# The first layer's convolution: from three element-wise engines to float32 products on TensorE

## The chip, the cores and the metric

One core of one Trainium2 chip runs the whole program. The metric is the device time of one execution in microseconds. A core has TensorE (PE in the profile; PEld are its weight loads), VectorE (DVE), ScalarE (ACT), GpSimd (POOL) and SyncE (SP, which issues most of the DMAs here). They run side by side and wait for each other by semaphores. Each takes its own instructions in the order in which the program lists them.

## The reference, cut to what matters

The model has two layers over 256 latent tokens and 256 context tokens, of width 1024. The first layer normalizes and modulates its input, projects it once, and splits the result into a convolution branch (values `a`, gates `g`, 512 channels each) and grouped-query attention (8 query heads, 2 key heads, of 64). Both results are joined and projected back.

```python
def _conv_branch(a, g, conv_w, ln_g, ln_b):
    y = a * jax.nn.sigmoid(g)
    pad = CONV_WIDTH // 2
    y = lax.conv_general_dilated(y, conv_w[:, None, :].astype(y.dtype), (1,), [(pad, pad)],
                                 dimension_numbers=('NWC', 'WIO', 'NWC'), feature_group_count=CONV_CH)
    return jax.nn.silu(_layer_norm(y, ln_g, ln_b))
...
    y_l = jnp.concatenate([conv_l, att_l], axis=-1) @ w_out
```

The convolution is per channel: 31 taps along the tokens, separately for latent and context tokens. The layer norm goes over the 512 channels of a token. After this come a dense SwiGLU, then the second layer with differential attention and a top-2-of-8 expert SwiGLU, and a last norm. All is float32.

## The kernel before, in words

Weights are streamed from HBM in tiles of 1 MB by `Stream`: `load` issues a DMA, `split` (ScalarE, L140) and `low` (VectorE, L152) make a rounded high part and a low part of a tile, and `mm3` (L222) forms a product as high x high, high x low and low x high, at the fast rate of the type F32R. `ws.step()` lets the stream split one tile more. `ws.get` forces splits until the wanted one is there. The DMAs and the splits go in the order in which a first pass over the program asks for the tiles.

The order of the work around the change is written out by hand in `build`:

1. The shifted, scaled input `hT` is made, and the first half of gates and values is projected with it (blocks j = 0, 1 of 128 channels); gated, they lie in `ypad` (128 channels x 4 blocks x 2 streams x 286 padded tokens).
2. The keys and values of the attention are projected (`kv_proj`), normed and rotated (`kv_a`, `kv_b`), and turned (`kv_T`).
3. The queries likewise, in four tiles of 128 tokens (`q_proj`, `q_a`, `q_b`, `q_T`).
4. Attention runs over 32 units (a tile of tokens and a head) in a software pipeline: scores (`ev_A`), maximum, exponential, transposes (`ev_C`), high and low parts, product with the values (`ev_D`), division by the sums (`ev_E`). The generator `ag1` puts the second half of gates and values (j = 2, 3) between these units. `fill` does the same with later adaLN rows, in `ada_half` (L334): float32 products with 32 output columns, in four column groups.
5. The output projection `w_out` takes eight blocks k of joined channels: 0 to 3 from the convolution, 4 to 7 from attention. It goes through them in the order kk = 2, 3, 0, 1 of pairs.

The convolution runs beside steps 2 to 4 on the element-wise engines. `conv_v` has taps 0 to 12 on VectorE, a multiply and add each:

```python
nc.vector.scalar_tensor_tensor(cacc[:, j], ypad[:, j, :, w:w + 256], cw[:, j, w:w + 1], cacc[:, j],
                               op0=OP.mult, op1=OP.add)
```

`conv_p` has taps 13 to 30: ScalarE makes the product (L581), GpSimd adds it (L599). The calls `conv(p, v)` scattered through the code say how many steps of either are issued there. Its layer norm (`conv_ln`) follows from inside the attention loop: transposes to tokens, bn_stats, scaling. The SiLU (`conv_silu`) comes with transposes back at the start of the output projection.

PSUM has eight banks, by tags: "mm" four, "tr" two, "av" and "ad" one each. A tag's next user waits until the one before has been read.

Of the kernel before, what the change touches and what calls it, by code (L numbers as in the profile page):

```python
# [10 lines left out]
F32 = mybir.dt.float32  # L11
# [3 lines left out]
OP = mybir.AluOpType  # L15
# [180 lines left out]
def build(nc, tc, a, out, order, dbg=None, stop=None):  # L196
# [5 lines left out]
    def T(shape, name, dt=F32, tag=None, bufs=1):  # L202
        return pool.tile(shape, dt, name=name, tag=tag or name, bufs=bufs)
# [65 lines left out]
    dq(rows[16:20], a["ev_ln_g"].rearrange("b (k p) -> (b k) p", p=128))  # L269
    dq(rows[20:24], a["ev_ln_b"].rearrange("b (k p) -> (b k) p", p=128))  # L270
# [275 lines left out]
    cacc = T([128, 4, 2, 256], "cacc", tag="cB")  # L546
    NP = 18
    cpool = {}

    ready = set()  # L550

    def conv_v():
        for j in range(4):
            while j not in ready:
                yield
            nc.vector.tensor_scalar(cacc[:, j], ypad[:, j, :, 0:256], cw[:, j, 0:1], None, op0=OP.mult)
            yield
            for w in range(1, 31 - NP):
                nc.vector.scalar_tensor_tensor(cacc[:, j], ypad[:, j, :, w:w + 256], cw[:, j, w:w + 1], cacc[:, j],
                                               op0=OP.mult, op1=OP.add)  # L560
                yield
            while (j, "done") not in cpool:
                yield
            nc.vector.tensor_tensor(cacc[:, j], cacc[:, j], cpool[j].rearrange("p (s n) -> p s n", s=2), op=OP.add)
            cpool[j, "added"] = True
            yield

    def conv_p():

        todo = [(j, w) for j in range(4) for w in range(31 - NP, 31)]  # L570
        cps = T([128, 2, 512], "cps", tag="s4")
        prod = {}

        def product(i):
            j, w = todo[i]
            first = w == 31 - NP
            if first or i % 2:
                o = pool.tile([128, 512], F32, name="cp", tag="ptlo" if first else "pthi", bufs=2)
            else:
                o = cps[:, i // 2 % 2]  # L580
            nc.scalar.activation(o.rearrange("p (s n) -> p s n", s=2), ypad[:, j, :, w:w + 256], AF.Copy,  # L581
                                 scale=cw[:, j, w:w + 1])
            if first:
                cpool[j] = o
            prod[i] = o

        made = 0
        for i, (j, w) in enumerate(todo):
            while made < min(i + 3, len(todo)):
                j1, w1 = todo[made]  # L590
                if w1 == 31 - NP and (j1 not in ready or j1 >= 2 and (j1 - 2, "added") not in cpool):
                    if made > i:
                        break
                    yield
                else:
                    product(made)
                    made += 1
            if w > 31 - NP:
                nc.gpsimd.tensor_tensor(cpool[j], cpool[j], prod.pop(i), op=OP.add)  # L599
            if w == 30:  # L600
                cpool[j, "done"] = True
            yield

    convg, convp = conv_v(), conv_p()

    def conv_rest():
        while run(convg, 1):
            run(convp, 2)

    def conv(p, v):  # L610
        return run(convp, p) | run(convg, v)

    def latent(p):
        return p.rearrange("p (s n) -> p s n", s=2)

# [3 lines left out]
    def gated(j, pa):  # L619

        y = ypad[:, j, :, 15:271]
        nc.vector.tensor_tensor(y, latent(pa), y, op=OP.mult)
        ready.add(j)
# [6 lines left out]
    def ag1():  # L630

        for i in (1, 0):
            u = ag_w(i, 1)
            for j in (2, 3):
                o = PS("ad")
                ag_mm(o, u, j, range(4))
                yield
                yield
                ag_mm(o, u, j, range(4, 8))
                if j == 3:  # L640
                    ws.done(("win", i, 1), 0, 1)
                yield
                (gate_to if i == 1 else gated)(j, o)
                yield

    ag2 = ag1()


# [25 lines left out]

    kT = [T([128, 2, 512], f"k{q}", F32R, tag=f"b{4 + q}") for q in range(2)]
# [83 lines left out]
    conv(2, 1)  # L759
# [3 lines left out]
    conv(1, 1)  # L763
# [4 lines left out]
    conv(1, 1)  # L768
# [3 lines left out]
    ws.fewer(spares)  # L772
    ws.done(("win", 3, 0), 0, 1)
    bq = [PS("av"), PS("mm"), PS("mm"), PS("mm")]
# [3 lines left out]
    conv(1, 1)  # L778
    kv_b(2)
    kv_a(3)  # L780
    q_proj(0)
    kv_b(3)
    conv(1, 0)
    q_a(0)
    kv_T(0)()
    conv(0, 1)
    q_b(0)
    conv(2, 1)
    q_proj(1)
    q_a(1)  # L790
    kv_T(2)()
    conv(0, 1)
    q_b(1)
    conv(2, 1)
    q_proj(2)
    q_a(2)
    q_T(0)()
    conv(0, 1)
    q_b(2)
    conv(2, 1)  # L800
    for k in range(8):
        mm3(bq[3], [x[:, k, 384:512] for x in hT], [x[:, k % 2, :] for x in un[k // 2]], k == 0, k == 7)
        if k % 2:
            ws.done(("win", 2, k // 4), k // 2 % 2)
            ws.step()
    q_a(3)
    q_T(1)()
# [13 lines left out]
    run(ag2, 4)  # L821
# [86 lines left out]
    yn = {}  # L908

    def conv_ln():  # L910
        yn[0] = T([128, 4, 512], "yn", tag="cA")
        mv = T([128, 4, 2], "mv")
        for t in range(4):
            p = PS("tr")
            for j in range(4):
                tr(p[:, j * 128:(j + 1) * 128], cacc[:, j, t // 2, (t % 2) * 128:(t % 2) * 128 + 128])
            yield
            nc.scalar.copy(yn[0][:, t], p)
            bs = SM(6, "bs")
            nc.vector.bn_stats(bs, p)  # L920
            nc.vector.bn_aggr(mv[:, t], bs)
            yield
        r = powm(mv[:, :, 1], 4, 1.0, 1e-5)
        yield
        for t in range(4):
            nc.vector.tensor_scalar(yn[0][:, t], yn[0][:, t], mv[:, t, 0:1], r[:, t:t + 1], op0=OP.subtract,
                                    op1=OP.mult)

    def conv_silu():
        for j in range(4):  # L930
            p = PS("tr")
            for t in range(4):
                tr(p[:, t * 128:(t + 1) * 128], yn[0][:, t, j * 128:(j + 1) * 128])
            cs = W("cs")
            nc.scalar.activation(cs, p, AF.Silu, scale=lnT[:, j:j + 1], bias=lnT[:, 4 + j:5 + j])
            parts(cat[0][:, j, :], cat[1][:, j, :], cs)
            yield

    ws.lag = 5
    lng = conv_ln()  # L940
    n = len(units)
    evs = None
    for i in range(n + 8):
        if 0 < i < 7:
            run(ag2, 1)
        if i < n:
            ev_A(i)
        if 3 <= i < n + 3:
            ev_C(i - 3)
        if 2 <= i < n + 2:  # L950
            ev_exp(i - 2)
        if evs is not None:
            run(evs, 1)
        if 1 <= i < n + 1:
            ev_max(i - 1)
        if 4 <= i < n + 4:
            ev_parts(i - 4)
        if 5 <= i < n + 5:
            ev_D(i - 5)
            if i % 4 == 0:  # L960
                evs = ev_E((i - 5) // 8, (i - 5) // 4 % 2)
        run(qlast, 1)
        ws.step()
        rest = conv(2, 1 + i % 2)
        if i < 6:
            run(ag2, 1)
        if i == 9:
            run(ag2)
            cat[:] = new_h("cat")
        if i >= 9:  # L970
            fill(2 if i >= 16 and i % 3 == 0 else 1)
        if i >= 34:
            conv_rest()
            rest = False
        if not rest:
            run(lng, 1 + i % 2)
# [4 lines left out]
    conv_rest()  # L981
    run(lng)
    fill(10 ** 6)
    ws.lag = 0
    sil = conv_silu()
# [14 lines left out]
    run(sil, 1)  # L1000
# [13 lines left out]
    for i, kk in enumerate((2, 3, 0, 1)):  # L1014
        un = w_out_w(0, kk)
        for t in range(4):
            w_out(0, kk, t, bo[t], un, i == 0, i == 3)
        ws.done(("wout", 0, 0, kk // 2), kk % 2)
        ws.step()
        run(sil, 2)  # L1020
        if i >= 1:
            run(gg, 2)
        fill(2)
# [3 lines left out]
    uns = {kk: w_out_w(1, kk) for kk in (2, 3, 0, 1)}  # L1027
    fillers += [ada_half(0, 5, 1)]
    for t in range(4):
        bank = PS("mm")  # L1030
        for i, kk in enumerate((2, 3, 0, 1)):
# [839 lines left out]
_INS = ['x', 'c', 'ctx', 'c_ctx', 'ada_b', 'norm1_g', 'norm2_g', 'ev_conv_w', 'ev_ln_g', 'ev_ln_b', 'ev_q_norm_g',  # L1871
# [13 lines left out]
def weights(v):  # L1885
# [8 lines left out]
    out["t_win"] = np.stack([wide[0:2], wide[2:4], q, np.stack([wide[6], wide[6]])])  # L1894
    wo = [blocks(v[n][0], 512, 512).transpose(1, 0, 2, 3) for n in ("ev_w_out", "od_w_out")]
# [51 lines left out]
```

## Time and profile before

| | us |
|---|---|
| median of 3 runs | 2074.19 (2070.69 to 2074.53) |
| profiled execution | 2073.23 |
| its span, first to last instruction | 2071.4 |
| TensorE busy | 1984.1 |
| VectorE busy | 1539.5 |
| ScalarE busy | 1185.9 |
| GpSimd busy | 336.1 |

The span is what the trace covers; the execution's own time is 1.8 us longer. Busy time counts only instructions that compute, and a matmul's end is modelled, so a busy TensorE is not one at its peak. [...]

### The profile page before, as it was taken

The page shows a single profiled execution, that of the slowest core. Times are in us where ns is not written, and L with a number is a line of the kernel's source. Part 1 is how long each engine was busy: PE and PEld are TensorE (multiplying, and loading weights), DVE is VectorE, ACT ScalarE, POOL GpSimd, SP SyncE. Part 2 cuts the span into 40 slices and gives each one's busy share as a digit, 9 for nine tenths or more (in the row PEclk, how much of TensorE's full clock was granted, in tenths as well). Part 3 has the DMA queues.
Part 4 walks back from the last instruction along what each step waited for, and adds up shares of the span by engine and source line. Part 5 has one row for each costly group of instructions (what it writes and reads, how often), then busy time and mean ns, then how long its engine had stood idle before and what let it go on. Part 6 is the DMA issues. An engine that isn't in the chain of part 4 may idle for free.

```text
span 2071.4 us, 26926 instructions
## 1 busy us (share of the span) xinstructions
PE 1984.1 (96%) x9910; PEld 1609.1 (78%) x9910; DVE 1539.5 (74%) x1965; ACT 1185.9 (57%) x1635; POOL 336.1 (16%) x285
## 2 busy tenths in 40 slices
PE   6999899999999998999999999999999999999987
PEld 4766677777777776889878888888888888888876
DVE  3789643545546466666559999999999999999997
ACT  3467433222222222434458888878788888888776
POOL 0568210333324243011110000000000000000020
PEclk9999699999999999999889999999999999999999
DMA  8315332333332223332397999999999999999972
GB/s 300 117 42 202 124 136 107 143 122 125 125 131 94 81 99 120 126 123 102 127 337 289 354 359 353 359 361 373 360 346 364 372 367 352 356 358 375 352 304 96
DMA packets 98632, 483.28 MB, mean 233 GB/s; under 512 B 12169, under 2 KB 12833, under 8 KB 51648
## 3 DMA queue, kind: packets, MB, share of 16 engines
q1 hardware_dynamic: 96128, 479.84, 62.7%
q10 hardware_dynamic: 2368, 1.68, 0.3%
q8 instruction: 79, 1.29, 0.3%
q14 instruction: 57, 0.47, 0.1%
HBM read 480.43 MB, written 1.05 MB: 232 GB/s over the span
## 4 chain that ended last, share of the span: by engine, by line
PE 57%; DVE 2%; ACT 1%; issue 0%; DVEq 0%; POOL 0%; ACTq 0%; POOLq 0%
PE mm L223 12%; PE mm L225 12%; PE mm L224 12%; PE av L224 3%; PE av L225 3%; PE av L223 3%; PE ad L225 2%; PE ad L223 2%; PE ad L224 2%; PE tr L308 2%; DVE wlo L152 1%; PE tr L1636 1%; PE tr L1562 1%; PE tr L1514 0%; PE av L1448 0%
## 5 line engine op out<-in xcount | busy, mean ns | idle before, releaser
L140 ACT CAST whi<-raw 128x1024 fp32r<-128x1024 f32 x420 | 434.7, 1049 | 232.8 <-PE tr L225 102.7
L152 DVE TENSOR_TENSOR wlo<-raw,whi 128x1024 fp32r<-128x1024 f32 x420 | 547.5, 1342 | 9.6 <-ACT whi L140 7.7
L224 PE MATMUL mm<-wlo,xghi 128*128 128x512 f32 x896 | 351.3, 392 | 5.1 <-DVE wlo L152 5.0
L223 PE MATMUL mm<-whi,xghi 128*128 128x512 f32 x896 | 354.6, 396 | 0.0
L225 PE MATMUL mm<-whi,xglo 128*128 128x512 f32 x896 | 351.2, 392 | 0.0
L990 POOL TENSOR_TENSOR x<-x,tmp 128x512 f32<-128x512 f32 x110 | 163.3, 1516 | 387.8 <-DVE tmp L989 356.8
L140 ACT CAST whi<-spare 128x512 fp32r<-128x512 f32 (+1 forms) x282 | 189.1, 709 | 45.0 <-PE mm L225 27.4
L152 DVE TENSOR_TENSOR wlo<-spare,whi 128x512 fp32r<-128x512 f32 (+1 forms) x282 | 212.3, 794 | 0.0
L224 PEld LDWEIGHTS mm<-wlo,xghi 128*128 128x128 f32 x896 | 168.9, 188 | 43.5 <-DVE wlo L152 8.4
L225 PEld LDWEIGHTS mm<-whi,xglo 128*128 128x128 f32 x896 | 168.7, 188 | 36.4
L223 PEld LDWEIGHTS mm<-whi,xghi 128*128 128x128 f32 x896 | 168.9, 188 | 34.6
L223 PE MATMUL mm<-h2hi,whi 128*128 128x512 f32 x448 | 178.2, 398 | 1.0 <-ACT h2hi L228 1.0
L224 PE MATMUL mm<-h2lo,whi 128*128 128x512 f32 x448 | 177.3, 396 | 0.6 <-DVE h2lo L229 0.5
L225 PE MATMUL mm<-h2hi,wlo 128*128 128x512 f32 x448 | 176.8, 395 | 0.0
L1088 DVE TENSOR_TENSOR silu<-mm,silu 128x512 f32<-128x512 f32 x28 | 19.4, 692 | 191.7 <-PE mm L225 191.7
L1649 POOL MEMSET fgain<- 128x1 f32 x1 | 0.1, 98 | 899.3 <-DVE wlo L152 899.3
L152 DVE TENSOR_TENSOR wlo<-rawx,whi 128x1024 fp32r<-128x1024 f32 x112 | 134.3, 1221 | 3.1 <-ACT whi L140 0.7
L140 ACT CAST whi<-rawx 128x1024 fp32r<-128x1024 f32 x112 | 117.4, 1052 | 31.0 <-PE mm L225 25.7
L223 PEld LDWEIGHTS mm<-h2hi,whi 128*128 128x128 f32 x448 | 84.0, 187 | 24.3 <-issue 3.4
L224 PEld LDWEIGHTS mm<-h2lo,whi 128*128 128x128 f32 x448 | 84.0, 188 | 21.5 <-DVE h2lo L229 1.6
L225 PEld LDWEIGHTS mm<-h2hi,wlo 128*128 128x128 f32 x448 | 84.1, 188 | 20.0
L223 PE MATMUL mm<-whi,h3hi 128*128 128x256 f32 x320 | 93.8, 293 | 1.3 <-ACT h3hi L228 1.3
(374 smaller groups left out, 4065.9 us busy)
## 6 DMA issues: line engine op xcount, KB each, us to landing
raw<-in_t_g_dram SPq DMA_DIRECT2D x81, 1024.0 KB, 7.1
rawx<-in_t_u_dram SPq DMA_DIRECT2D x53, 1024.0 KB, 7.2
raw<-in_t_ada_dram SPq DMA_DIRECT2D x38, 1024.0 KB, 4.9
raw<-in_t_u_dram SPq DMA_DIRECT2D x30, 1024.0 KB, 7.4
raw<-in_t_d_dram SPq DMA_DIRECT2D x30, 1024.0 KB, 7.2
spare<-in_t_g_dram SPq DMA_DIRECT2D x56, 512.0 KB, 7.0
spare<-in_t_u_dram SPq DMA_DIRECT2D x112, 256.0 KB, 6.8
rawb<-in_t_d_dram SPq DMA_DIRECT2D x27, 1024.0 KB, 7.3
```

The lines of the kernel that those rows point to most:

```text
L140: self.nc.scalar.copy(hi[:, i * n:(i + 1) * n], x)
L152: self.nc.vector.tensor_tensor(lo[:, c], x, hi[:, c].bitcast(F32), op=OP.subtract)
L223: mm(o, L[0], R[0], start=first, stop=False)
L224: mm(o, L[0], R[1], start=False, stop=False)
L225: mm(o, L[1], R[0], start=False, stop=last)
L308: nc.tensor.transpose(o, i, ident[:i.shape[0], :i.shape[0]])
L990: (eng or nc.gpsimd).tensor_tensor(X[t][:, c0:c1], X[t][:, c0:c1], tmp, op=OP.add)
L1088: nc.vector.tensor_tensor(sg[j], p, sg[j], op=OP.mult)
L1562: mm(p[:, i * 256:i * 256 + 256], x[:, t, k * 128:k * 128 + 128], S[:, t].rearrange("p j n -> p (j n)"), start=n == 0 and t == 0, stop=n = ...
L1636: mm(p, PT[:, t * 128:(t + 1) * 128], hl[q][:, o * 512:(o + 1) * 512], start=q == 0, stop=q == 1)
L1649: nc.gpsimd.memset(fgain[0][:, 0:1], 0.0)
```

## The change

The convolution becomes matrix products. For each tap w and each block j of 128 channels, `conv_weights` makes on GpSimd a diagonal: for every quadrant g of 32 partitions a 32x32 matrix with the tap's weights on the diagonal. `conv` then issues, for each tap, 16 float32 products (4 blocks x 4 quadrants) of 32 rows, 32 columns and 512 tokens, which accumulate over the 31 taps in four PSUM banks, the four "mm" banks. Quadrant g of block j goes to the partitions of quadrant (g + j) mod 4 of bank j, so that the 16 products of one tap use 16 different pairs of row and column quadrant. The channels come out turned by j quadrants in block j; the norm's gains and biases (`t_ln`, now one input and one DMA instead of two) and the rows of the output projection's weights are turned alike on the host.

`ag1` is no longer a generator: all gates and values are done before the keys. The taps come after the key projections, in five portions (6, 6, 6, 6, 7) with the keys' norm, rotation and transposes between them. ScalarE copies the four banks to `cacc`. The norm and the SiLU run between the steps of the query tiles (`ln_rows`, `ln_scale`, `ln_cols`), the result `cs` waits in SBUF, and the attention loop makes its high and low parts. The joined tile `cat` is made at the start of the loop, `fill` begins at i = 6 instead of 9, and the output projection takes kk in the order 0, 1, 2, 3.

```diff
-    dq(rows[16:20], a["ev_ln_g"].rearrange("b (k p) -> (b k) p", p=128))
-    dq(rows[20:24], a["ev_ln_b"].rearrange("b (k p) -> (b k) p", p=128))
+    dq(rows[16:24], a["t_ln"])
...
-    cacc = T([128, 4, 2, 256], "cacc", tag="cB")
-    NP = 18
-    def conv_v():
...
-    def conv_p():
...
+    diag = T([128, 32], "diag")
+    nc.vector.tensor_reduce(diag, ident.rearrange("p (g i) -> p i g", g=4), op=OP.add, axis=AX.X)
+    def conv_weights():
+        t = T([128, 2, 31, 32], "dg", tag="cB")
+        u = T([128, 31, 32], "dgu", tag="s4")
+        v = [pool.tile([128, n, 32], F32, name="dgv", tag="ptlo", bufs=2) for n in (16, 15)]
+        for j in range(4):
+            for w0, d in ((0, (t[:, 0], t[:, 1], u)[j]),) if j < 3 else ((0, v[0]), (16, v[1])):
+                n = d.shape[1]
+                nc.gpsimd.tensor_tensor(d, diag.unsqueeze(1).to_broadcast([128, n, 32]),
+                                        cw[:, j, w0:w0 + n].unsqueeze(2).to_broadcast([128, n, 32]), op=OP.mult)
...
+    def conv():
+        bc4.extend(PS("mm") for _ in range(4))
+        for w in range(31):
+            for j in range(4):
+                for g in range(4):
+                    c, r = slice(32 * ((g + j) % 4), 32 * ((g + j) % 4) + 32), slice(32 * g, 32 * g + 32)
+                    mm(bc4[j][c].rearrange("p (s n) -> p s n", s=2), dgs[j, w][r], ypad[r, j, :, w:w + 256],
+                       start=w == 0, stop=w == 30)
+            yield
...
+    ag1()
...
+    conv_weights()
...
     kv_proj(3)
     kv_b(1)
     kv_a(2)
-    ws.fewer(spares)
     ws.done(("win", 3, 0), 0, 1)
+    ws.step()
+    cv = conv()
+    run(cv, 6)
+    kv_b(2)
+    kv_a(3)
+    ws.step()
+    run(cv, 6)
+    kv_b(3)
+    ws.step()
+    run(cv, 6)
+    kv_T(0)()
+    ws.step()
+    run(cv, 6)
+    ws.step()
+    run(cv)
+    kv_T(2)()
+    cacc = T([128, 4, 2, 256], "cacc", tag="cB")
+    for j in range(4):
+        nc.scalar.copy(cacc[:, j].rearrange("p s n -> p (s n)"), bc4[j])
...
     q_proj(0)
     q_a(0)
+    ln_rows(0)
     q_b(0)
+    ln_rows(1)
     q_proj(1)
     q_a(1)
+    ln_rows(2)
+    ln_rows(3)
+    lr = powm(mv[:, :, 1], 4, 1.0, 1e-5)
     q_b(1)
+    q_T(0)()
     q_proj(2)
+    ln_scale(lr, range(4))
     q_a(2)
+    q_T(1)()
     q_b(2)
+    cs = T([128, 4, 512], "cs", tag="cB")
     for k in range(8):
         mm3(bq[3], [x[:, k, 384:512] for x in hT], [x[:, k % 2, :] for x in un[k // 2]], k == 0, k == 7)
         if k % 2:
             ws.done(("win", 2, k // 4), k // 2 % 2)
             ws.step()
+            ln_cols(k // 2)
     q_a(3)
...
-    for i, kk in enumerate((2, 3, 0, 1)):
+    for i, kk in enumerate((0, 1, 2, 3)):
```

## Rows read from the trace of the kernel before

**Rows 1.** The page: busy shares, granted clock in tenths, the chain's engines.

```profile
PE 1984.1 (96%) x9910; PEld 1609.1 (78%) x9910; DVE 1539.5 (74%) x1965; ACT 1185.9 (57%) x1635; POOL 336.1 (16%) x285
...
PEclk9999699999999999999889999999999999999999
...
PE 57%; DVE 2%; ACT 1%; issue 0%; DVEq 0%; POOL 0%; ACTq 0%; POOLq 0%
```

**Rows 2.** Windows: us; busy PE PEld DVE ACT POOL; clock, DMA, GB/s.

```profile
101.56:111.80 10.24, 5.02 (x11) 3.54 (x12) 9.29 (x14) 6.51 (x10) 5.21 (x4) 0.50 0.16 46
...
180.07:183.48 3.41, 3.41 (x20) 1.96 (x23) 3.37 (x4) 1.83 (x5) 3.22 (x3) 0.50 0.00 0
...
207.37:214.20 6.83, 6.28 (x29) 3.02 (x28) 6.76 (x8) 5.14 (x13) 5.69 (x5) 0.50 0.15 28
...
221.03:251.75 30.72, 25.65 (x101) 21.91 (x101) 17.55 (x42) 12.86 (x28) 1.07 (x2) 0.50 0.32 117
sum 188.37, PE 169.83 PEld 130.86 DVE 158.60 ACT 109.07 POOL 111.47; mean PE 21.23 PEld 16.36 DVE 19.82 ACT 13.63 POOL 13.93
```

**Rows 3.** TensorE's waits, 63.38 to 251.75: us in total, times, longest.

```profile
PE av L223 <- DVE on L898: 3.7, 3, 1.6
PE ad L223 <- ACT whi L140: 3.6, 1, 3.6
...
PE ad L225 <- DVE wlo L152: 2.2, 1, 2.2
```

**Rows 4.** Groups by line, 63.38 to 247.4: xcount | busy us, mean ns.

```profile
L559 DVE SCALAR_TENSOR_TENSOR cacc<-ypad,cw,cacc 128x512 f32<-128x512 f32 x48 | 60.3, 1257 | 0.5
...
L581 ACT ACTIVATE cp<-ypad,cw 128x512 f32<-128x512 f32 x40 | 28.5, 722 | 2.0 <-POOL cp L599 2.0
L581 ACT ACTIVATE cps<-ypad,cw 128x512 f32<-128x512 f32 x32 | 23.5, 735 | 1.7 <-POOL cp L599 1.7
...
L599 POOL TENSOR_TENSOR cp<-cp 128x512 f32<-128x512 f32 x36 | 56.0, 1555 | 12.6 <-ACT cp L581 10.3
```

**Rows 5.** The windows again, in the odd layer.

```profile
835.42:1002.68 167.26, 164.34 (x1353) 150.75 (x1352) 106.33 (x236) 69.97 (x130) 16.53 (x16) 1.00 0.33 120
1002.68:1016.33 13.65, 12.62 (x48) 9.44 (x48) 11.42 (x29) 7.32 (x17) 3.31 (x9) 0.50 0.50 158
```

**Rows 6.** Line L334, 153.0 to 155.1: ns min/median/max, first and last start.

```profile
L334 PE MATMUL ad<-raw,s x16: 592/592/617, 153.1 to 154.4; 128*32 128x512 f32 x16
```

**Rows 7.** Windows with L334's instructions alone.

```profile
153.30:153.40 0.10, 0.10 (x4) 0.00 (x0) 1.00 0.00 0
```

**Rows 8.** TensorE in order of time, odd layer: start us, us, what.

```profile
996.23 0.50 PE L223 MATMUL mm<-k,qall 64*128 64x512 f32 x2
996.56 0.39 PE L224 MATMUL mm<-k,qall 64*128 64x512 f32 x2
996.79 0.40 PE L225 MATMUL mm<-k,qall 64*128 64x512 f32 x2
```

**Rows 9.** The page, part 5: GpSimd's costliest group.

```profile
L990 POOL TENSOR_TENSOR x<-x,tmp 128x512 f32<-128x512 f32 x110 | 163.3, 1516 | 387.8 <-DVE tmp L989 356.8
```

**Rows 10.** Groups by line again: the steps of norm and queries.

```profile
L920 DVE BATCH_NORM_STATS2 bs<-tr 128x6 f32<-128x512 f32 x4 | 2.8, 698 | 7.9 <-ACT yn L918 7.9
L736 DVE TENSOR_REDUCE sm<-sq 128x8 f32<-128x512 f32 x4 | 2.7, 676 | 0.0
...
L734 ACT ACTIVATE sq<-mm 128x512 f32<-128x512 f32 x3 | 1.8, 596 | 2.9 <-DVE sm L736 2.2 <-PE mm L225 0.7
```

**Rows 11.** TensorE in order of time, first layer; [idle before <-releaser].

```profile
179.42 0.30 PE L223 MATMUL av<-v,pt 128*128 128x128 f32 x1 [1.04 <-DVE on L898]
...
244.83 0.69 PE L308 MATMUL mm<-ident,on 128*128 128x128 f32 x2 [1.26 <-DVE on L898]
...
255.01 1.03 PE L308 MATMUL tr<-ident,yn 128*128 128x128 f32 x8
```

**Rows 12.** Line L270 on SP's queue.

```profile
L270 SPq DMA_DIRECT2D rows<-in_ev_ln_b_dram x1: 295/295/295, 2.3 to 2.3; - x1
```

More of the change, by code (lines that the diff above doesn't have):

```diff
@@ L545, in build @@
     nc.vector.tensor_copy(cw, p.rearrange("p (j w) -> p j w", j=4)[:, :, 0:31])
-    cacc = T([128, 4, 2, 256], "cacc", tag="cB")
-    NP = 18
-    cpool = {}
-    ready = set()
-    def conv_v():
[L553 to L566, printed above, removed]
@@ L568, in conv_p @@
-    def conv_p():
[L570 to L611, printed above, removed]
     def latent(p):
         return p.rearrange("p (s n) -> p s n", s=2)
+    diag = T([128, 32], "diag")
+    nc.vector.tensor_reduce(diag, ident.rearrange("p (g i) -> p i g", g=4), op=OP.add, axis=AX.X)
+    dgs = {}
+    def conv_weights():
[7 more added lines that the diff above has]
+                                        cw[:, j, w0:w0 + n].unsqueeze(2).to_broadcast([128, n, 32]), op=OP.mult)
+                for w in range(n):
+                    dgs[j, w0 + w] = d[:, w]
@@ L616, in gate_to @@
+    bc4 = []
+    def conv():
[7 more added lines that the diff above has]
+            yield
     def gate_to(j, pg):
@@ L622, in gated @@
         nc.vector.tensor_tensor(y, latent(pa), y, op=OP.mult)
-        ready.add(j)
     for j in range(2):
@@ L634, in ag1 @@
             for j in (2, 3):
-                o = PS("ad")
+                o = PS(("ad", "av")[j % 2])
                 ag_mm(o, u, j, range(4))
-                yield
-                yield
+                ws.step()
                 ag_mm(o, u, j, range(4, 8))
                 if j == 3:
+                    ws.fewer(spares)
                     ws.done(("win", i, 1), 0, 1)
-                yield
+                ws.step()
                 (gate_to if i == 1 else gated)(j, o)
-                yield
-    ag2 = ag1()
+    ag1()
     CSG = T([128, 2, 2, 2, 64], "CSG")
@@ L758, in build @@
     ws.step()
-    conv(2, 1)
     kv_proj(1)
@@ L762, in build @@
     ws.step()
-    conv(1, 1)
     kv_proj(2)
@@ L767, in build @@
     ws.step()
-    conv(1, 1)
     kv_proj(3)
@@ L771, in build @@
     kv_a(2)
-    ws.fewer(spares)
     ws.done(("win", 3, 0), 0, 1)
-    bq = [PS("av"), PS("mm"), PS("mm"), PS("mm")]
+    ws.step()
[9 more added lines that the diff above has]
+    kv_T(0)()
+    ws.step()
+    run(cv, 6)
+    ws.step()
+    run(cv)
[3 more added lines that the diff above has]
+        nc.scalar.copy(cacc[:, j].rearrange("p s n -> p (s n)"), bc4[j])
+    bq = [PS("av"), PS("ad"), PS("mm"), PS("mm")]
     un = [[t.rearrange("p (k n) -> p k n", k=2) for t in ws.get(("win", 2, i // 2), i % 2)] for i in range(4)]
@@ L777, in build, with ln_rows, ln_scale, ln_cols @@
     qT = [[T([128, 2, 512], f"q{q}{g}", F32R, tag=f"b{q * 2 + g}") for g in range(2)] for q in range(2)]
-    conv(1, 1)
-    kv_b(2)
-    kv_a(3)
+    yn = T([128, 4, 512], "yn", tag="cA")
+    mv = T([128, 4, 2], "mv")
+    def ln_rows(t):
+        p = PS("tr")
+        for j in range(4):
+            tr(p[:, j * 128:(j + 1) * 128], cacc[:, j, t // 2, (t % 2) * 128:(t % 2) * 128 + 128])
+        nc.scalar.copy(yn[:, t], p)
+        bs = SM(6, "bs")
+        nc.vector.bn_stats(bs, p)
+        nc.vector.bn_aggr(mv[:, t], bs)
+    def ln_scale(r, ts):
+        for t in ts:
+            nc.vector.tensor_scalar(yn[:, t], yn[:, t], mv[:, t, 0:1], r[:, t:t + 1], op0=OP.subtract, op1=OP.mult)
+    def ln_cols(j):
+        p = PS("tr")
+        for t in range(4):
+            tr(p[:, t * 128:(t + 1) * 128], yn[:, t, j * 128:(j + 1) * 128])
+        nc.scalar.activation(cs[:, j], p, AF.Silu, scale=lnT[:, j:j + 1], bias=lnT[:, 4 + j:5 + j])
     q_proj(0)
-    kv_b(3)
-    conv(1, 0)
     q_a(0)
-    kv_T(0)()
-    conv(0, 1)
+    ln_rows(0)
     q_b(0)
-    conv(2, 1)
+    ln_rows(1)
     q_proj(1)
     q_a(1)
-    kv_T(2)()
-    conv(0, 1)
+    ln_rows(2)
+    ln_rows(3)
+    lr = powm(mv[:, :, 1], 4, 1.0, 1e-5)
     q_b(1)
-    conv(2, 1)
+    q_T(0)()
     q_proj(2)
+    ln_scale(lr, range(4))
     q_a(2)
-    q_T(0)()
-    conv(0, 1)
+    q_T(1)()
     q_b(2)
-    conv(2, 1)
+    cs = T([128, 4, 512], "cs", tag="cB")
     for k in range(8):
@@ L805, in build @@
             ws.step()
+            ln_cols(k // 2)
     q_a(3)
-    q_T(1)()
     def q_last():
@@ L820, in build @@
     qlast = q_last()
-    run(ag2, 4)
     cat = []
@@ L906, in ev_E @@
         yield
[L908 to L937, printed above, removed]
     ws.lag = 5
-    lng = conv_ln()
+    cat[:] = new_h("cat")
     n = len(units)
@@ L943, in build @@
     for i in range(n + 8):
-        if 0 < i < 7:
-            run(ag2, 1)
         if i < n:
@@ L963, in build @@
         ws.step()
[L964 to L976, printed above, removed]
+        if 8 <= i < 16 and i % 2:
+            j = (i - 8) // 2
+            parts(cat[0][:, j, :], cat[1][:, j, :], cs[:, j])
+        if i >= 6:
+            fill(1)
     dump("ypad", ypad)
@@ L980, in build @@
     dump("cathi", cat[0].bitcast(F32))
-    conv_rest()
-    run(lng)
     fill(10 ** 6)
     ws.lag = 0
-    sil = conv_silu()
     def residual(t, c0, c1, ps, g, eng=None):
@@ L999, in build @@
     fillers += [ada_half(0, 5, 0)]
-    run(sil, 1)
     xn = xn_tiles(4)
@@ L1019, in build @@
         ws.step()
-        run(sil, 2)
         if i >= 1:
@@ L1026, in build @@
     fill(10 ** 6)
-    uns = {kk: w_out_w(1, kk) for kk in (2, 3, 0, 1)}
+    uns = {kk: w_out_w(1, kk) for kk in (0, 1, 2, 3)}
     fillers += [ada_half(0, 5, 1)]
@@ L1030, in build @@
         bank = PS("mm")
-        for i, kk in enumerate((2, 3, 0, 1)):
+        for i, kk in enumerate((0, 1, 2, 3)):
             w_out(1, kk, t, bank, uns[kk], i == 0, i == 3)
@@ L1868, in build @@
     return ws
-_INS = ['x', 'c', 'ctx', 'c_ctx', 'ada_b', 'norm1_g', 'norm2_g', 'ev_conv_w', 'ev_ln_g', 'ev_ln_b', 'ev_q_norm_g',
+_INS = ['x', 'c', 'ctx', 'c_ctx', 'ada_b', 'norm1_g', 'norm2_g', 'ev_conv_w', 'ev_q_norm_g',
         'ev_k_norm_g', 'od_lam', 'od_subln_g', 'od_router_w', 'final_norm_g']
@@ L1894, in weights @@
     out["t_win"] = np.stack([wide[0:2], wide[2:4], q, np.stack([wide[6], wide[6]])])
+    turn = np.arange(512).reshape(4, 4, 32)
+    turn = np.stack([np.roll(turn[j], j, 0) for j in range(4)]).reshape(512)
+    out["t_ln"] = np.concatenate([v[n][0][turn].reshape(4, 128) for n in ("ev_ln_g", "ev_ln_b")])
+    v = dict(v)
+    v["ev_w_out"] = np.concatenate([v["ev_w_out"][:, turn], v["ev_w_out"][:, 512:]], 1)
     wo = [blocks(v[n][0], 512, 512).transpose(1, 0, 2, 3) for n in ("ev_w_out", "od_w_out")]
```

## The prediction

> **What bounds the kernel now.** I read the page first: TensorE is busy 96% of the span and holds 57% of the chain that ended last [rows 1]. So a microsecond counts only if it is a microsecond of TensorE: work, waiting, or time at the slower clock. The line of granted clocks tells where to look: tenths of 9 and 8 everywhere but for a 6 in the fifth slice [rows 1]. Of 51.8 us each, it is 207 to 259 us: the end of the first layer's attention. The convolution runs beside this layer's projections and attention on three other engines.
>
> Next I cut that stretch, from the end of the gate and value projections (63.4 us) to the first products of the output projection (251.75 us), at the changes of the granted clock [rows 2]. [...] Over all eight pieces it was busy 169.83 of 188.37 us: 18.5 us idle. A matmul is counted to its modelled end, some 0.16 us after the next could have started (0.39 us long, issued every 0.23, [rows 8]), so each of the dozen gaps hides a little more: about 1.5 us, a choice. **Lost in the stretch: 20.2 + 18.5 + 1.5 = 40 us.** Its work at full clock and without gaps is 148 us.
>
> Who caused it: the waits name VectorE's `on`, and the casts and subtractions of late weight tiles (L140, L152) [rows 3]. These instructions are short; they were late because they stood in queues behind the convolution. It holds VectorE for 60.3 us at L559 alone, ScalarE for 28.5 + 23.5 us, GpSimd for 56.0 us with half of its additions [rows 4]. What the stretch looks like without a convolution is seen in the odd layer: 167 us of projections and attention at granted clock 1.00, TensorE busy 164.3 of them [rows 5].
>
> **The change, part by part.**
>
> *Removed:* 56 VectorE instructions, 72 on ScalarE, 68 on GpSimd. All were off TensorE; their removal is worth what TensorE lost by them, at most 40 us.
>
> *Added on TensorE:* 31 taps x 4 blocks j x 4 quadrants g = 496 products, float32, 32x32 by 512 columns. The trace has float32 products of 512 columns with 32 output columns: `ada_half` calls 8, and the row counts 16 matmuls, so a call is two passes; 992 passes here. Each lasts 592 ns, but 16 begin between 153.1 and 154.4 [rows 6], and in each tenth of a microsecond four are in flight [rows 7]: four at once (one for each group of 32 output columns), three steps in 1.3 us, 0.43 us a step. So the chip runs passes on different columns of the array together, though a call's second pass has to wait for its first. [...] The 16 products of one tap use all 16 pairs of row and column quadrant. Bounds: all 16 at once, 992/16 x 0.43 = 26.7 us; four at once, as the nearest row has it, 106.6 us; one at a time 427 us. I take 16, since rows and columns each show it, and 1.3 us for fill and drain around the two transposes: **+28 us**.
>
> [...]
>
> *Diagonals:* five GpSimd products of 3968 elements per partition in all. The nearest GpSimd row does 512 in 1516 ns [rows 9], so 11.7 us; if contended twice that. They are issued before the key projections, and 33 us of TensorE work (the rest of the gates, the keys) lie before the first tap: hidden. Without that cover they would cost their 12 us.
>
> *Moved forward:* the second half of the gates and values (4 x 24 matmuls, some 22 us) goes from between the scores to before the keys: the same work. Its weight tiles now precede those of keys and queries in the DMA order, so the forced cast and subtraction at 104.55 and 108.0 (3.6 + 2.2 us, in rows 3) go.
>
> *Copies out of PSUM:* four on ScalarE, about 0.6 us each as L734, which reads a bank too [rows 10]; the first query projection (5.5 us) needs none of them. Hidden; without that cover 2.4 us. The norm's 32 transposes cost TensorE what they cost before. Twelve of them came behind 251.75 us, eight of these in 1.03 us [rows 11], and come earlier now: no net cost. The output projection's order of k only suits what is ready first.
>
> *What is late next.* (a) `q_T(0)` needs a "tr" bank that `ln_rows(2)` holds until bn_stats; before it on VectorE stands `q_a(1)`: square 0.60, reduction 0.68, bn_stats 0.70 = 2.0 us after the projection [rows 10], less 1.0 us for eight transposes [rows 11]: 1.0 us, and 0.3 for the small steps between; `q_proj(2)` is queued behind. (b) The first softmax waits for the backlog of the last query tile (square, reduce, power, gain, a subtraction, the maximum, the exponential, some 5 to 6 us by estimate from rows 10), TensorE having four scores of three products and two turned tiles, some 4 us: 1.5 us. (c) The last `on`, 1.26 us before [rows 11], stays at about 1 us. Together 4 us. A gap costs more than itself: the one of 1.04 us at 179.42 [rows 11] was followed by 3.41 us at 0.50 [rows 2]. Between no such piece and three of 3.4 us (each half lost): 0 to 5 us; I take 3. **Left: 7 us.**
>
> *Start:* one DMA issue less on SP's queue, 295 ns [rows 12], ahead of the first weights: 0.3 us gained at most, 0 at least; I take 0.3.
>
> **Sum.** -40 + 28 + 7 - 0.3 = -5 us. The profiled execution took 2073.23 us (span 2071.4 and 1.8 around it); 2068 for it. The median of the runs shown is 2074.19, 1 us above: **2069 us**.
>
> **The rivals.**
>
> *Stalls return (other side).* Same convolution, but the norm puts 4 bn_stats, 4 scalings and 8 more PSUM turns into a stage in which VectorE has the queries' norm and rotation too. If gaps (a) to (c) each bring a piece of 10.2 us at half clock, as 101.56 to 111.80 did [rows 2], the loss is 4 + 3 x 4.5 = 17.5 us: 2073.2 + 1 - 40 + 28 + 17.5 = 2080. It decides from 12 us of loss on: there the gain is gone. For it: even the odd layer has 13.65 us at half clock in its last units [rows 5]. Against it: VectorE loses 60.3 of its 158.6 us in the stretch.
>
> *Fewer at once.* Eight passes together, since a call's second pass stands between the firsts and only so many calls are looked ahead, give 124 x 0.43 = 53 us: 2069 + 26 = 2095; twelve give 36 us: 2078. A clock halved during the taps would cost the same 26. For it: no row shows more than four. Against it: with four, each step fills at once.
>
> [...]
>
> *All of the loss goes:* no gap of a microsecond left, as in the odd layer's 167 us: 7 us less, 2062.
>
> *The freed engines were not the cause,* and the gaps stay: 2102. Against it: the waits name these engines, and the odd layer runs clean. Counted with "fewer".
>
> **How the numbers follow.** Chances: forecast 0.54 (its own range 2060 to 2079), stalls 0.18, fewer at once 0.11, four at once 0.07, all gone 0.10. A change of 0.2% (4 us, what repeated runs can tell) sets the bounds at 2070 and 2078. Faster: 0.33 of the forecast and all 0.10 of the last; the same: 0.19 of the forecast and 0.07 of the stalls; slower: the rest, 0.31. The range leaves out four at once, the worst of fewer and a part of the last: 2056 to 2093.
>
> **What would show it.** Taps: 992 passes within 27 to 30 us, 16 in flight, clock 1.00; at four in flight the forecast is wrong. VectorE, ScalarE, GpSimd without L559, L581, L599. The first score near 155 us (63.4, and 22 + 11 + 28 + 26 us of gates, keys, taps and queries with the norm, and 4 for small things), the first product of the output projection near 246 us and at full clock, with no transposes of the norm behind it. Half-clock pieces between 63 and 250 us below 10 us in all instead of 51. If the sum of gaps and half-clock loss there is over 12 us, the kernel is not faster.

## The result and the profile after

The changed kernel takes **2090.14 us** (median of 4 runs, 2088.74 to 2090.92), the kernel before 2074.36 in the same comparison: ratio 1.0077, 95% interval 1.0059 to 1.0094. It is 16 us slower, where the prediction had 5 us gained (2069). The profiled execution took 2090.47 us (span 2088.7), 17.2 more than that of before.

The page of the changed kernel: busy shares, the granted clock in tenths of TensorE's full speed, the chain's engines.

```profile
PE 2013.3 (96%) x10902; PEld 1625.5 (78%) x10902; DVE 1470.8 (70%) x1910; ACT 1145.8 (55%) x1568; POOL 245.2 (12%) x222
...
PEclk9998999999999999999879999999999999999999
...
PE 57%; DVE 2%; ACT 1%; issue 0%; DMA 0%; DVEq 0%; POOL 0%; ACTq 0%; POOLq 0%
```

Against [rows 1] the 6 in the fifth slice has become an 8 in the fourth, and VectorE, ScalarE and GpSimd have 69, 40 and 91 us less to do: the engines were freed and the clock at the end of the attention came back, as meant. TensorE is busy 29 us longer.

Windows of the same stretch (to the first product of the output projection), cut where the granted clock changes:

```profile
63.79:165.53 101.74, 97.63 (x1341) 74.85 (x1341) 41.20 (x84) 23.44 (x41) 20.80 (x14) 1.00 0.13 43
165.53:186.01 20.48, 19.57 (x72) 12.82 (x72) 9.19 (x16) 7.71 (x20) 0.00 (x0) 0.50 0.03 5
186.01:259.15 73.14, 72.00 (x544) 55.93 (x540) 40.27 (x96) 38.79 (x101) 0.00 (x0) 1.00 0.55 204
```

One piece at half clock is left of the four in [rows 2]: 19.57 busy us in it, so 9.8 lost. (A score's last two products start 0.43 us apart in it, at 167.71 and 168.14, and 0.23 us apart at 1.00, at 162.32 and 162.55, so a busy microsecond there is counted half as lost.) Idle are 4.1 + 0.9 + 1.1 = 6.2 us. Together 16 us, where the prediction left 7. The waits of that stretch:

```profile
PE tr L307 <- DVE qr L657: 3.2, 1, 3.2
PE tr L307 <- DVE bs L765: 1.2, 1, 1.2
PE mm L307 <- DVE on L892: 0.5, 1, 0.5
```

They answer to [rows 3]. One wait of 3.2 us is the largest, and the half clock begins within it. TensorE around it, in order of time:

```profile
159.73 0.39 PE L225 MATMUL mm<-whi,hTlo 128*128 128x512 f32 x1
...
160.82 0.41 PE L224 MATMUL mm<-k,q 64*128 64x512 f32 x2
161.06 0.40 PE L225 MATMUL mm<-k,q 64*128 64x512 f32 x2
...
162.32 0.39 PE L224 MATMUL mm<-k,q 64*128 64x512 f32 x1
162.55 0.39 PE L225 MATMUL mm<-k,q 64*128 64x512 f32 x1
166.10 1.08 PE L307 MATMUL tr<-ident,qr 128*128 128x128 f32 x4 [3.17 <-DVE qr L657]
```

And VectorE's queue in the same microseconds:

```profile
161.90 0.69 DVE L698 TENSOR_REDUCE sm<-sq 128x8 f32<-128x512 f32 x1 [4.29 <-ACT sq L696]
162.62 0.17 DVE L382 TENSOR_SCALAR v<-sm 128x8 f32<-128x8 f32 x1
164.54 0.69 DVE L653 TENSOR_TENSOR qn<-mm,r 128x512 f32<-128x512 f32 x1 [1.75 <-POOL r L384]
165.26 0.69 DVE L657 TENSOR_TENSOR qr<-qn,gq 128x512 f32<-128x512 f32 x1
165.87 1.28 DVE L831 TENSOR_REDUCE nm<-mm 128x1 f32<-128x512 f32 x2
```

`q_b(3)` waits 1.75 us on GpSimd's power. TensorE's next transposes, those of the last query tile, need its result `qr`, and the first maximum stands behind it too. Matching products of the two traces show where the 17.2 us arise (times of the kernel before): 11.7 at the first product of the output projection (247.4 became 259.1), 8.4 at 264 (between the two, the kernel before still had 4.4 us at half clock and twelve of the norm's turns to do), 9.0 at 1017. From there on two things are added that the prediction has no term for. The clock, after and then before:

```profile
1059.82:1083.71 23.89, 23.15 (x101) 19.18 (x102) 6.66 (x29) 8.64 (x18) 4.86 (x4) 0.50 0.90 346
```

```profile
1050.46:1064.12 13.66, 13.44 (x63) 10.05 (x62) 4.27 (x17) 4.16 (x7) 4.85 (x4) 0.50 0.89 324
...
1067.53:1074.36 6.83, 6.83 (x24) 5.86 (x24) 2.72 (x4) 5.81 (x12) 0.00 (x0) 0.50 0.95 395
```

One piece of 23.9 us instead of two of 20.5 together; 23.15 - 13.44 - 6.83 = 2.9 busy us more, half of them lost: 1.4 us. That makes 10.4 us at 1085. And a drift from there to 16.9 at 2031, at granted clock 1.00. It sits in the products whose weights are the tile `hF` (duration min/median/max), first the changed kernel's, then the first of before's, whose six medians are all 389:

```profile
L223 PE MATMUL av<-whi,hF x224: 388/395/482, 1105.9 to 2072.4; 128*128 128x512 f32 x112
L224 PE MATMUL av<-wlo,hF x224: 387/393/497, 1106.2 to 2072.7; 128*128 128x512 f32 x112
L225 PE MATMUL av<-whi,hF x224: 389/396/404, 1106.4 to 2072.9; 128*128 128x512 f32 x112
L223 PE MATMUL ad<-whi,hF x224: 387/392/404, 1106.7 to 2073.8; 128*128 128x512 f32 x112
L224 PE MATMUL ad<-wlo,hF x224: 389/393/404, 1106.9 to 2074.0; 128*128 128x512 f32 x112
L225 PE MATMUL ad<-whi,hF x224: 388/392/404, 1107.2 to 2074.3; 128*128 128x512 f32 x112
```

```profile
L223 PE MATMUL av<-whi,hF x224: 388/389/486, 1095.6 to 2055.3; 128*128 128x512 f32 x112
```

6 + 4 + 7 + 3 + 4 + 3 = 27 ns, by 224: 6.0 us by the medians. The same instructions on the same data; what differs is where `hF` lies: the change allocates the 128 bytes of `diag` and the 4096 bytes of tag s4 ahead of tags b5 to b7, so b7, where `hF` lives, begins 4224 bytes higher.

The taps last, TensorE in order of time, the groups on block 3 alone (one row for each of a tap's two passes of four products):

```profile
103.09 0.67 PE L575 MATMUL mm<-ypad,dgv 32*32 32x512 f32 x4
...
103.54 0.64 PE L575 MATMUL mm<-ypad,dgv 32*32 32x512 f32 x4
...
104.15 0.66 PE L575 MATMUL mm<-ypad,dgv 32*32 32x512 f32 x4
...
104.60 0.64 PE L575 MATMUL mm<-ypad,dgv 32*32 32x512 f32 x4
```

From a first pass to its second 0.45 us, as forecast; from there to the next tap's first 0.61. A tap takes 1.05 us instead of 0.86, the whole from 97.59 to 131.97, 34.4 us with the keys' four turns among them.

### The profile page after: what moved, and what is told of

The parts are those of the page before. It is cut to its first block, busy times and chain, and to the rows that moved or that the text cites. A ratio compares the mean times of both kernels' runs of the same rounds, so it can differ in the third digit from the quotient of the medians.

```text
span 2088.7 us, 28689 instructions
## 1 busy us (share of the span) xinstructions
PE 2013.3 (96%) x10902; PEld 1625.5 (78%) x10902; DVE 1470.8 (70%) x1910; ACT 1145.8 (55%) x1568; POOL 245.2 (12%) x222
## 3 DMA queue, kind: packets, MB, share of 16 engines
HBM read 480.43 MB, written 1.05 MB: 231 GB/s over the span
## 4 chain that ended last, share of the span: by engine, by line
PE 57%; DVE 2%; ACT 1%; issue 0%; DMA 0%; DVEq 0%; SPq 0%; POOL 0%; ACTq 0%; POOLq 0%
PE mm L223 12%; PE mm L225 12%; PE mm L224 12%; PE av L225 3%; PE av L224 3%; PE av L223 3%; PE ad L223 2%; PE ad L225 2%; PE ad L224 2%; PE tr L307 2%; DVE wlo L152 1%; PE tr L1584 1%; PE tr L1510 1%; PE tr L1462 1%; PE av L1396 0%
```

## The experiments

Ratios are against the kernel before, run beside each.

**The price of the taps.** One tap instead of 31.

> The changed kernel with one tap of the convolution, 30 of 31 left out: what TensorE pays for them. If the taps cost what the trace of the changed kernel shows between them, 1.045 us each and 2 us at two stops, 33 us go: 2090 becomes 2057. By the prediction's 0.86 us each and 27 us in all: 2063. If the taps cover work of VectorE for the keys that then comes into the open, fewer than 20 us go: above 2070. The wait for the last query tile's rotation (3.2 us) and 20 us of half clock behind it should stay in all three.

2060.43 us (0.9944, 0.9929 to 0.9959): 30 us less for 30 taps. From the first tap to the output projection the trace is 27.2 us shorter, but a new wait stands in it, with a short piece at half clock behind it:

```profile
PE tr L307 <- DVE kw L653: 3.2, 1, 3.2
```

```profile
103.65:107.06 3.41, 3.41 (x9) 2.63 (x8) 1.46 (x3) 2.31 (x5) 0.00 (x0) 0.50 0.64 187
```

The keys' turns wait for their rotation, which the taps had covered. With 3.5 us of waiting (0.3 of it on a second step of the rotation) and 1.7 lost to the clock, the 30 taps are 32.4 us, all 31 some 33 to 34. The rest of the 30 us is clock in the last layer, whose pieces are shorter here as in `place`, next.

**Addresses.**

```diff
-    diag = T([128, 32], "diag")
+    diag = W("diag", 32)
...
-    conv_weights()
     kT = [T([128, 2, 512], f"k{q}", F32R, tag=f"b{4 + q}") for q in range(2)]
     vv = [T([128, 4, 2, 64], f"v{q}", F32R, tag=f"b{6 + q}") for q in range(2)]
+    conv_weights()
```

> The changed kernel with the large SBUF tiles back at the addresses of the kernel before (two allocations in another order, the 128 bytes of the diagonal in a tile of the ring that holds scratch rows); no instruction is added or removed. Theory placement: the 1315 products of the last layer with hF as weights go from 232.5 back to 228 ns, and the time falls by 6 us to 2084. Rival: the slower products come from the chip or the run and not from the address: 2090, and 232.5 ns stays.

2080.77 us (1.0043, 1.0029 to 1.0057), 9.4 less than the changed kernel, and the products are back at 389:

```profile
L223 PE MATMUL av<-whi,hF x224: 388/389/486, 1101.7 to 2061.5; 128*128 128x512 f32 x112
```

The other way round, in the kernel before: 128 bytes more, and the s4 tile allocated ahead of b5 to b7.

> The kernel before, with the SBUF tiles of the later layers moved as the change moves them (128 bytes more and one tile of 4096 bytes allocated earlier; one short memset on GpSimd is added). Theory placement: the products of the last layer with hF as weights take 232.5 instead of 227.8 ns; 1334 of them make 6.4 us: 2073 + 6 = 2079. Rival: the address matters only together with the change: 2073.

2079.24 us (1.0034, 1.0023 to 1.0045), 6.2 more, with the changed kernel's medians:

```profile
L223 PE MATMUL av<-whi,hF x224: 388/395/482, 1092.5 to 2058.8; 128*128 128x512 f32 x112
```

So 6 us of the 16 have nothing to do with the convolution's work. The 3 us more that `place` gained stand in its clock: two pieces of half clock further on are 3.4 us shorter each. `late_q3` below, with its tiles where the change put them, has the same two shorter pieces, so the addresses aren't their cause; what is stays open.

**Why a tap takes 1.05 us.** The products in another order; and only half of them.

```diff
-            for j in range(4):
-                for g in range(4):
+            for g in range(4):
+                for j in range(4):
```

> The changed kernel with the 16 products of a tap in another order: the four blocks of one row quarter follow each other, instead of the four row quarters of one block. Theory order: two of the 16 lag behind the others by half a pass, which makes five half passes (1.045 us) of four; in another order they would not, a tap takes 0.87 us and the time falls by 5 us to 2085. Rival: the sixteen weight loads between two steps set the 0.19 us, whatever the order: 1.045 us stays, 2090. If products into one bank had to take turns, this order would be the faster one, since neighbours write different banks.

2088.9 us in a single run, the taps still 33.7 us from first to last start: the order is not it.

> The changed kernel with only two of the four channel blocks convolved (taps 1 to 30 of blocks 2 and 3 left out): 8 of the 16 products per tap. Theory issue: TensorE's queue holds the next tap back because 32 weight loads and 32 products per tap go through it in order; with half as many a tap takes its two passes of 0.43 us, 0.87 us, and the time falls by 5 us. Rival: a step between two taps costs 0.19 us in itself: 1.045 us stays. Were the products run one behind the other in a bank, a tap would take half as long.

2082.2 us in a single run. TensorE in order of time, the taps behind the keys' turns:

```profile
114.69 11.40 PE L575 MATMUL mm<-ypad,dg 32*32 32x512 f32 x208
```

208 passes are 13 taps; without the last pass's modelled tail (0.16 us) 11.24 / 13 = 0.86 us each. Eight products in a tap keep the pace of the two passes, sixteen (1.05 us) don't. Twelve are in `hybrid2`, below.

**The wait of 3.2 us and the half clock behind it.** First the rotation behind the maxima.

```diff
     def q_last():
-        q_b(3)
-        yield
         e = q_T(2)
         yield
         e()
+        yield
+        q_b(3)
+        yield
+        yield
         e = q_T(3)
```

> The changed kernel with the last query tile's gain moved behind the first two maxima on VectorE's queue and its transposes two units later on TensorE's. Theory late query tile: the wait of 3.2 us and the 20 us at half clock behind it (9.5 us lost) go together: 2090 - 12 = 2078. Rival: only the wait goes and the clock falls all the same: 2087. Second rival: the first softmax is bounded by other work of the queue and the gap stays: 2090.

2086.39 us (1.0069, 1.0056 to 1.0083). From the first tap to the first product of the output projection 161.2 us against 161.5: nothing gained, the wait has only changed its name (the profiled run is 5.1 us faster by 1.8 ahead of the first tap and by the shorter pieces in the last layer):

```profile
PE mm L223 <- DVE qn L653: 3.0, 1, 3.0
```

The score of the fourth unit (i = 3) needs a bank that holds the last query projection until `q_b(3)` has read it. So, with `place`, that projection went to the av bank (`bq.append(PS("av"))`):

> The kernel with the tiles back at their addresses, with two more edits: the last query tile's rotation behind the first two maxima, as tried alone, and its projection into the bank of the first query tile (tag av) instead of one of the four that the scores use. Theory bank: late_q3 only swapped the wait, since the scores of the third unit need the bank that VectorE frees with the first step of that rotation; with both edits no score waits, the 3 us go and with them the 20.5 us at half clock (about 9.5 us lost): 2081 - 12 = 2069. Rival: the clock falls in this stretch whatever stands before it: 2078. Second rival: the gap moves on to the exponential behind its table load: 2081.

2081.44 us (1.0053, 1.0032 to 1.0074), no gain on `place` in all. The stretch from the first tap to the output projection is 2.0 us shorter than there, with 17.1 us at half clock behind a wait of

```profile
PE tr L307 <- ACT p L840: 2.6, 1, 2.6
```

the first exponential, which stood behind an evacuation of `q_T(2)` (163.79) and a table load of 1.28 us (164.18). Moving the first query tile's turns behind the third projection takes the 1.15 us wait away, but 0.5 us on the norm's scaling and 0.4 on the evacuation of a query tile come in its place, as the rival has it:

> As bank, and the first query tile's transposes behind the third query projection instead of ahead of it, so that they don't wait for the norm's statistics (1.15 us). Theory: 1.2 us less than bank: 2068, and faster than the kernel before (2073). Rival: the wait moves to the norm's scaling or the next transposes: as bank.

2080.01 us (1.004, 1.0027 to 1.0053). Then everything of the last query tile went behind the first exponentials, and its projection into the ad bank:

```diff
     def q_last():
-        q_b(3)
-        yield
         e = q_T(2)
         yield
+        yield
         e()
+        yield
+        q_a(3)
+        yield
+        yield
+        q_b(3)
+        yield
         e = q_T(3)
```

> As bank_t0, with the first softmax freed at last: the square, the sum and the rotation of the last query tile go behind the first exponentials (its projection into the ad bank, which is free longer), and the evacuation of the third query tile behind the first exponential. In bank_t0 the first exponential stood on ScalarE behind an evacuation and a table load of 1.28 us, and TensorE waited 2.6 us for it; 17 us at half clock followed all the same. Theory gap: with no gap of a microsecond between 140 and 170 us the clock stays at 1.00 there, 2.6 + 8.5 us go: 2080 - 11 = 2069. Rival clock: the half clock comes from this stretch as such, and only the gap goes: 2077. Second rival: the gap moves once more, to a bank or to the next maximum: 2080.

2076.54 us (1.0011, 1.0001 to 1.0021): 3.5 of the hoped-for 11. A wait of 1.1 us is left, and 10.2 us at half clock:

```profile
PE tr L307 <- DVE pt L229: 1.4, 2, 1.1
```

```profile
171.11:181.35 10.24, 10.24 (x42) 6.00 (x42) 4.22 (x8) 2.67 (x7) 0.00 (x0) 0.50 0.11 24
```

**Fewer products on TensorE, the rest on the idle VectorE.**

> As soft, with 6 of the 31 taps on VectorE (24 instructions, one beside each of TensorE's first 24 taps; its sums are added where the banks are evacuated). Theory: VectorE is mostly idle beside the taps, 6 taps of 1.045 us go from TensorE: 6 us less than soft, 2063 by the gap theory, and the fastest of all. Rival: VectorE is late again, as in the kernel before: its 24 instructions of about 1.26 us (30 us) hold back the keys' rotation and the first query tile, and soft and hybrid come out the same or hybrid slower.

2065.67 us (0.9965, 0.9952 to 0.9978): 11 less than soft, more than the 6 us of taps. The kernel leaves out the turn by quadrants of VectorE's sums, so it is not yet the whole convolution. The same wait of 1.06 us, and behind it no half clock:

```profile
161.33:184.00 22.67, 22.67 (x167) 16.72 (x168) 13.92 (x26) 12.76 (x31) 0.47 (x1) 1.00 0.33 115
```

This trace is of the fastest of its five runs (2062.27 us, granted clock 0.990 over the whole span; the others 0.980 to 0.989). Its pieces at half clock are shorter even in layers that the edit doesn't touch: 6.8 us at 818 and at 998, where `soft` has 10.2 each. So that no half clock follows here may be the run and not the kernel.

> As soft, with 24 of the 31 taps of channel block 0 on VectorE, one instruction beside each of TensorE's first 24 taps, so that 24 of the taps on TensorE have 12 products instead of 16 (in hybrid the sums were taken for all blocks without the rotation by 32 partitions that the products give blocks 1 to 3, so its values were off, not its work); the last query tile's square and rotation one unit later still. Theory issue: with 12 products a tap takes its two passes, 0.87 us, as with 8, so the taps take 28 instead of 34 us, and soft's 2076 becomes 2070; if the last wait of 1.06 us and the 10 us at half clock behind it go as well, 2065. Rival: the tap's time goes with the products (0.065 us each, 0.78 for 12): 27 us, hardly to be told apart by the time, but by the steps. Second rival: the pace stays 1.045 with 12: 34 us, 2076.

2076.38 us (1.0016, 1.0002 to 1.0029). The pace came as the issue theory has it. Rows of block 3's first passes in two of the seven taps of 16 ahead, 1.06 us apart, then, in the same trace, both passes of its taps of 12, 0.86 us from one first pass to the next:

```profile
100.44 0.66 PE L575 MATMUL mm<-ypad,dgv 32*32 32x512 f32 x4
...
101.50 0.66 PE L575 MATMUL mm<-ypad,dgv 32*32 32x512 f32 x4
...
104.00 0.64 PE L575 MATMUL mm<-ypad,dgv 32*32 32x512 f32 x4
...
104.44 0.64 PE L575 MATMUL mm<-ypad,dgv 32*32 32x512 f32 x4
...
104.86 0.64 PE L575 MATMUL mm<-ypad,dgv 32*32 32x512 f32 x4
...
105.29 0.64 PE L575 MATMUL mm<-ypad,dgv 32*32 32x512 f32 x4
```

The taps ran from 96.0 to 125.0, but the time did not follow: 13.7 us at half clock behind a wait of 0.84 us, and 10.2 more behind a new one of 1.4 us at the end of the attention, probably because the modulation's fillers, begun one unit later, now meet the last `on`'s there (not tested).

```profile
163.67:177.32 13.65, 13.65 (x58) 10.16 (x61) 6.60 (x12) 4.55 (x11) 0.94 (x1) 0.50 0.01 1
```

> As soft, with 9 of the 31 taps of all four blocks on VectorE (36 instructions of about 0.78 us as they took in hybrid, 28 us in all, 12 of them beside the key projections), and one more step of 16 products on TensorE that adds VectorE's sums into the banks, through the stacked 32x32 identity, so that they get the rotation by 32 partitions. TensorE then has 23 steps of 1.02 us instead of 31, some 24 instead of 34 us. Theory: the taps are what is left to be had, soft's 2076.5 becomes 2067, and 2062 if no half clock follows the first softmax, as it was with hybrid. Rival: VectorE, with 28 us more in a stretch of 60, holds up the keys, whose turns wait as the weights' and the scores' did in the kernel before, and the clock falls: 2075. The kernel before: 2073.

2070.59 us (0.999, 0.9981 to 0.9999). The rival had a part of it: TensorE waited for VectorE's last sum,

```profile
PE mm L583 <- DVE part L595: 3.7, 1, 3.7
```

and behind it a short piece at half clock, besides 10.2 us of it at the first softmax:

```profile
127.23:130.64 3.41, 2.89 (x13) 1.23 (x14) 0.46 (x1) 0.00 (x0) 0.00 (x0) 0.50 0.00 0
```

**Does the wait make the half clock?** Two kernels that differ in the last query tile alone, in its place and in the bank and tile that go with it: `hybrid4` is `hybrid3` with 8 taps on VectorE, `hybrid4_wait` the same with the tile's work ahead of the first softmax.

> As hybrid3, with 8 instead of 9 taps on VectorE (32 instructions, 24 steps of 16 products on TensorE). In hybrid3 TensorE waited 3.7 us for VectorE's last sum; four instructions of 0.78 us fewer take 3.1 us off that wait and one step of 1.04 us comes back: 2070.6 - 2 = 2068.5. If the half clock behind the first softmax (10 us in hybrid3) stays away as in hybrid: 2063.

> hybrid4 with the last query tile's work where the change had it, ahead of the first softmax: nothing else differs. Theory gap: the wait of 3.2 us comes back and behind it some 20 us at half clock, as in the changed kernel, against 10 us or none: 2 us more of waiting and 5 to 9 us of clock, 2068.5 becomes 2076 to 2080. Rival: the half clock depends on the work before (the convolution's passes) and not on the wait: only the 2 us come, 2070.5.

`hybrid4` takes **2068.90 us (0.9974, 0.9961 to 0.9988)**, the fastest version with the whole convolution, 21 us less than the change and 3.7 less than before. `hybrid4_wait` takes 2073.98 (1.0013, 1.0004 to 1.0022), 5.1 more. First `hybrid4`, its wait and the half clock behind it, then `hybrid4_wait`:

```profile
PE tr L307 <- DVE pt L229: 2.4, 3, 1.1
```

```profile
162.12:172.36 10.24, 10.24 (x44) 6.07 (x43) 4.39 (x8) 2.50 (x7) 0.00 (x0) 0.50 0.10 14
```

```profile
PE tr L307 <- DVE qr L677: 3.2, 1, 3.2
```

```profile
158.88:179.36 20.48, 19.80 (x72) 12.61 (x71) 8.24 (x15) 8.07 (x21) 0.00 (x0) 0.50 0.05 11
```

2.1 us more of waiting bring 10.2 us more at half clock (9.6 of them busy, so 4.8 lost); the product that opens the output projection comes 5.8 us later. By the medians the late tile costs 5.1 us, less than the gap theory's 7.5 to 11.5 and more than the rival's 2. Behind the 3.2 us the half clock is as long as in the changed kernel (20.5 us), with 24 steps on TensorE before it instead of 31, so the convolution before it doesn't set it; one trace of each shows this.

But the wait alone doesn't set it either. The 3.2 us of `one_tap` and the 3.7 us of `hybrid3`, with the query projection behind them instead of the softmax's scores and turns, were followed by 3.4 us; `hybrid2`'s 0.84 us at the softmax by 13.7. What decides, and why 1.06 us there was followed by 10 us (`soft`, `hybrid3`, `hybrid4`) or by none (`hybrid`), stays open; runs of `hybrid4` between 2059 and 2073 us, with a granted clock of 0.990 to 0.978, say that it changes from run to run.

## Why the prediction was wrong

**"At most 40 us" removed: right.** The 20.2 us in it are half of the 40.4 us that TensorE was busy in the four pieces at 0.50 of [rows 2]; the 18.5 are what it was idle of the eight pieces. The waits on the late weight tiles and the half clock of [rows 2, 3] are gone; the stretch before the taps (63.79 to 97.59) has no gap, and behind the softmax's start only gaps of 0.5 us and less are left.

**"16 at once, 0.43 us a step: +28 us": the first term that failed, 34.4 us.** Before the change no row shows sixteen at once: [rows 7] have four, on different columns, and the step from there was the author's estimate. That different rows run together the changed kernel's scores show: pairs of 64-row products start 0.24 us apart (160.82, 161.06), single ones 0.23 (162.32, 162.55). The sixteen do run together (32 passes in 1.05 us, where four in flight, at the 0.43 us a step of [rows 6], would need an estimated 3.4), and the quadrants of a block share their bank, but between two taps 0.16 to 0.19 us are lost, and with 8 or 12 products in a tap (0.86 us) they aren't. The rival "fewer at once" supposed a limited look ahead, between a call's two passes, which no run shows; what was lost stands between taps, and its cause is not shown.

A tap of 16 is 32 weight loads and 32 products, a tap of 12 is 24 of each. The measured paces, 1.05 and 0.86 us, don't contradict the issue theory, that their number holds the next tap back; no run here shows it.

Products into one bank that took turns would have made a tap of eight products in two banks, 16 passes, take eight turns of 0.43 us, an estimated 3.4 us. It took 0.86: row quadrants on different partitions of a bank don't take turns here.

**"Left: 7 us": the second, 16 us.** Gap (a) was 1.15 us, as forecast (1.3), gap (c) 0.5 (1.0). Gap (b) had the right place and backlog (6.0 us, from the last projection's end at 160.12 to 166.10), but not the cover: of the four scores and two turned tiles that were to fill 4 us only three scores and one tile stand ahead of the tile that waits, 2.4 us, and 0.4 of the norm's last turns. So 3.2 us instead of 1.5, and a piece at half clock of 20.5 us instead of up to three of 3.4: 9.8 us lost where 3 were taken. This is the rival "stalls return", with 16 of its 17.5 us, in one piece.

**The sum over the first layer**: -40 + 34.4 + 16 = +10; the traces show 8.4 at 264 us. Nothing else in the stretch cost anything: the diagonals, the gates moved forward and the four copies were hidden as worked out.

**Not in the sum at all: 6 us of placement** (shown both ways) and 1.4 us of clock at the last layer's start. The prediction asked what each edit does on each engine, and not what a new tile does to the addresses of those behind it. Without the placement the change would still be slower, by 8 us.

The mark set in advance held: a loss over 12 us between 63 and 250 us, and the kernel is not faster. The other signs point to the same two terms: the first score came at 160.5 us instead of near 155, the output projection at 259.1 instead of 246, after 20.5 us at half clock instead of less than 10. That 2090 lies within the stated range, up to 2093, is luck: that end stands for fewer passes at once, and 6 us came from outside the sum.

## What to carry to other kernels

A late tile can cost its wait and more in the clock behind it (here 9.8 us behind 3.2, but 1.7 behind an equal wait ahead of a projection), and the wait only goes when the whole chain is moved: here VectorE's queue, then the PSUM bank, then ScalarE's table load stood behind a wait of about the same 3 us (3.2, 3.0 and 2.6). Before counting cover, list what stands ahead of the waiting instruction in program order, not all the work that is at hand. After a change look for a small equal difference in instructions that it doesn't touch: it may come from where its tiles pushed others (here 3 to 7 ns a product, 6 us in all).

## What the runs showed of the hardware

- Products of 128x512 take 389 or 392 to 396 ns by where the tile of their weights lies in SBUF (4224 bytes apart, its neighbours moved with it), shown both ways (`place`, `before_shift`); why that address is the slower one is open.
- A tap's sixteen float32 products of 32x32, on 16 pairs of row and column quadrant, ran together: two passes of each in 1.05 us, and in 0.86 us with 8 or 12 products in a tap. A call's two passes don't follow each other directly: the first passes of block 3's four quadrants start within 0.05 us, and their second passes come 0.45 us later, behind first passes of other quadrants.
- Waits of 3.2, 2.6, 1.06 and 0.84 us at the first softmax were followed by 20.5, 17.1, 10.2 (once none) and 13.7 us at granted clock 0.50, waits of 3.2 and 3.7 us ahead of the query projection by 3.4 us.
